# Five operations of a decoder layer kernel moved to other places in their engines' queues

## The chip, the cores and the metric

The kernel runs on one core of a Trainium2 chip. The metric is the device time of one execution in microseconds (us). The kernel before took 818.10 us (median of three runs, 817.72 to 818.36).

A core has five engines, each with its own queue of instructions that is worked off in order: TensorE (PE, matrix products; its loading of weights is shown apart as PEld), VectorE (DVE), ScalarE (ACT), GpSimd (POOL) and SyncE (SP, which here only starts DMA transfers). An engine waits for another by a semaphore. A wait holds back everything behind it in that engine's queue.

## The reference

One layer of a decoder, for 512 tokens of width 1024, in float32:

```python
proj = x @ w_in                                  # q | k | v (3 groups x 8 heads x 64) | ssm input (512) | gates
for g, (window, dilation) in enumerate(DILATION_GROUPS):       # (128,1), (512,4), (2048,16)
    o_g, lse_g = dilated_group_attention(rope(q)[g], rope(k)[g], v[g], window, dilation)
attn = sum(softmax(lses) * outs);  y_attn = attn @ w_attn_br
y_s = s5_ssm(u, ...)                             # complex diagonal state space, scan over the tokens
y_s = glu(gelu(y_s) @ w_glu);      y_ssm = y_s @ w_ssm_br
mixed = sigmoid(gates[0]) * y_attn + sigmoid(gates[1]) * y_ssm
h = layer_norm(ALPHA * x + mixed @ w_out)
ff = (silu(h @ w_ff_gate) * (h @ w_ff_up)) @ w_ff_down
out = layer_norm(ALPHA * h + ff)
```

## The kernel before

Every matrix product of float32 data is made of three products of reduced numbers. A number is split into a high part (a cast to a shorter format, on ACT: names ending in `h`, `_hi` or `whi`) and a low part (the number less its high part, a subtraction on DVE: `l`, `_lo`, `wlo`), and PE adds high x high, high x low and low x high into one PSUM bank. A weight therefore goes through a DMA into a raw buffer, a cast on ACT and a subtraction on DVE before PE can use it. A class `Weights` does this in the order of use, one 128x1024 half at a time; a finished product releases its slot, and the release queues the next half's cast and subtraction. `w.flush()` emits a subtraction that has been put off.

The order of the work is written out by hand. Python code emits instructions product by product, and a table of steps (`at_step`) says at which product other pieces (the state space, scores, norms) are put in between. Each engine's queue holds its instructions in the order of emission. There is no scheduler.

The places that the change touches, in order of time:

**The first product** (`u_tiles`, line L613). Input and weights arrive in eight k-slices of 512 columns. A loop splits each slice: ACT casts the input (`x_hi`) and then the weight (`wuh`), DVE subtracts (`x_lo`, `wul`). Between slices DVE takes a few of the state space's small operations (`late.take`; their tiles are `t16s`, their line is L79). Slice 0 was split in halves ahead of the loop.

**The state space's output** (`ssm_out`, `ssm_gelu`). It is made in two rounds. `ssm_out(rnd)` is a short burst of products in the middle of a projection's product: `yt` (banks 3, 4; L724) and `yc` (banks 5, 6; L732). `ssm_gelu(rnd)` is emitted half a step later, behind that projection's own evictions: ACT copies `yt` into `ysb`, DVE adds `yc` to it, and the GELU follows on ACT and DVE. Both rounds use the same four banks. Between them on DVE stand the rotary products of one eviction (`kq`, `zk`) and a weight's subtraction (`wlo`).

**The values of the far groups** (`v_product(n, u)`, L1213). These are seven products of a Strassen scheme, in the order n = 1, 5, 2, 6, 3, 7, 4, each in two halves u. A half is 12 matmuls of 128x512 into two banks (e = 0, 1), with two k-slices and three terms. The input's forms are made on the way: form 5 is an `x_hi`, `x_lo` pair that is cast on ACT and subtracted on DVE; forms 6 and 7 (`x23h`, `x23l`) need a DMA that adds into `xf`. After the second half `v_evict(n)` copies or adds the banks out.

**The last of the quads** (`quad_product(j, n)`, L1257; j = 0 to 4, n in the order 1, 5, 6, 2, 7, 3, 4). Products 1, 6, 7 and 4 add up in one bank. After each, `quad_evict` reads what the bank holds. In the last quad the reading of product 7 is an addition to `qssw` on DVE (L348) and two tanh activations on ACT (L1268). In the loop the slot's release stands ahead of this reading, so the next weight's cast and subtraction are queued first.

**The last norm.** The 512 tokens are four tiles of 128. A tile's norm takes its two halves of 512 columns, with two operations on each: `norm_first` is (z - mean) * gain, `norm_second` is z * rstd + bias, both on DVE (L345). For tiles 0 and 1 the second half is shared out (`normalize_shared`): ACT computes z * rstd + nm, where `nm` = -mean * rstd, and POOL multiplies by the gain (L1457) and adds the bias (L1458). `rstd` is computed on POOL (L1431). For tile 2 all four operations are DVE's; in front of them in time is tile 3's first quarter, behind them the rest of tile 3 (`dnv`, the last product's bank), its norm and the last stores.

Of the kernel before, what the change touches and what calls it, by code (L numbers as in the profile page):

```python
# [10 lines left out]
F32 = mybir.dt.float32  # L11
F32R = mybir.dt.float32r
I32 = mybir.dt.int32
AF = mybir.ActivationFunctionType
ALU = mybir.AluOpType

P = 128
# [19 lines left out]
QUADS = [(1, 0), (1, 1), (2, 0), (2, 1), (None, 3)]  # L37
# [136 lines left out]
def emit(ctx, tc, i, out):  # L174
    nc = tc.nc
    pe, dve, act, pool, sp = nc.tensor, nc.vector, nc.scalar, nc.gpsimd, nc.sync
# [22 lines left out]
    def split(hi, lo, src, scale=None):  # L199
        if scale is None:  # L200
            act.copy(hi, src)  # L201
            dve.tensor_tensor(lo, src, hi.bitcast(F32), op=ALU.subtract)  # L202
        else:
            act.mul(hi, src, scale)
            dve.scalar_tensor_tensor(lo, src, scale, hi.bitcast(F32), op0=ALU.mult, op1=ALU.subtract)
# [18 lines left out]
    at = pa_ctx.enter_context(tc.tile_pool(name="at", bufs=2))  # L224
# [12 lines left out]
    def gat(n, name, dt=F32):  # L237
        return pa.tile([P, 2048], dt, tag=f"gat{n}", name=name)
# [13 lines left out]
    for n in range(2, N_GLU, 2):  # L252
        kind, g, un, _ = STEPS[n]
# [43 lines left out]
    for n, c in enumerate(cols256):  # L297

        xs, us = (raws[0][:, 0, 2 * n + e] for e in range(2))
# [29 lines left out]
    late = Later(dve)  # L329
# [8 lines left out]
    def ts(o, a, s1, op0, s2=None, op1=None, eng=dve):  # L338
        if s2 is None:
            eng.tensor_scalar(o, a, s1, None, op0=op0)  # L340
        else:
            eng.tensor_scalar(o, a, s1, s2, op0=op0, op1=op1)

    def stt(o, a, s1, b, op0, op1, eng=dve):
        eng.scalar_tensor_tensor(o, a, s1, b, op0=op0, op1=op1)  # L345

    def tt(o, a, b, op, eng=dve):
        eng.tensor_tensor(o, a, b, op=op)  # L348
# [148 lines left out]
    for k in range(KT):  # L497
        (xh, uh), (xl, ul) = ((z[k // 4][:, k % 4, :] for z in (xp[n], wup[n])) for n in range(2))
        raw = raws[k // 2][:, k % 2]
        if k == 0:  # L500
            late.take(4)
            continue
        for n, (hi, lo) in enumerate(((xh, xl), (uh, ul))):
            split(hi, lo, raw[:, 2 * n : 2 * n + 2].rearrange("p e c -> p (e c)"))
        late.take(4 if k < 2 else 10)


    xt = []
# [36 lines left out]
    ssm = {}  # L545
# [165 lines left out]
    def ssm_out(rnd):  # L711

        if rnd == 0:
            late.take(1000)
            ssm["ysb"] = gat(0, "ysb").rearrange("p (a i b c) -> p a i b c", a=2, i=4, b=2)
        ut, h, y = ssm["ut"], ssm["h"], ssm["ysb"]
        tb, cb = ([ring_(f"y{n}{rnd}{e}").rearrange("p (o i c) -> p o i c", o=2, i=2) for e in range(2)]
                  for ring_, n in ((scores, "t"), (turned, "c")))
        for e in range(2):
            for par in range(2):  # L720
                for half, rows in halves64:
                    for x, cols in halves64:
                        i_ = 4 * rnd + 2 * e + x
                        pe.matmul(tb[half][cols, par, e], ssm["tm"][rows, 2 * i_ + par, :], ut[rows, 2 * i_ + par, :],  # L724
                                  start=True, stop=True)
        for e in range(2):
            for half in range(2):
                for r in range(2):
                    for par, rows in halves64:
                        for x, cols in halves64:  # L730
                            i_ = 4 * rnd + 2 * e + x
                            pe.matmul(cb[par][cols, half, e], caf[rows, i_, r, half, :], h[r][rows, 2 * i_ + half, :],  # L732
                                      start=(r == 0), stop=(r == 1))
        ssm["yb"] = tb, cb

    def ssm_gelu(rnd):
        y, (tb, cb) = ssm["ysb"], ssm["yb"]
        is_ = slice(2 * rnd, 2 * rnd + 2)
        yf = [y[:, half, is_].rearrange("p i b c -> p (i b c)") for half in range(2)]
        y2 = [at.tile([P, 512], F32, tag="un", name=f"y2_{rnd}{half}", bufs=4) for half in range(2)]  # L740
        for half in range(2):
            for par in range(2):
                act.copy(y[:, half, is_, par], tb[half][:, par])
                tt(y[:, half, is_, par], y[:, half, is_, par], cb[par][:, half], ALU.add)
        for a, b in zip(y2, yf):
            act.square(a, b)
            ts(a, a, 0.044715, ALU.mult, 1.0, ALU.add)
            tt(a, a, b, ALU.mult)
        for a, b in zip(y2, yf):
            act.activation(a, a, AF.Tanh, scale=math.sqrt(2.0 / math.pi))  # L750
            stt(b, a, 1.0, b, ALU.add, ALU.mult)
# [452 lines left out]
    def v_product(n, u):  # L1204
        key = {1: "x", 6: "x", 7: "x", 4: "x", 2: "y", 5: "z", 3: "z"}[n]
        first = n in (1, 2, 5) and u == 0
        if first:
            vbank[key] = [bank(b, f"v{key}{b}") for b in {"x": (0, 7), "y": (1, 2), "z": (5, 6)}[key]]
        ws, xs = vops.pop((n, u)), forms_x["f"][n]
        for e in range(2):  # L1210
            for kk in range(2):
                for m, (p_, q_) in enumerate(((0, 0), (0, 1), (1, 0))):
                    pe.matmul(vbank[key][e], xs[p_][:, 2 * u + kk, 128 * e : 128 * e + 128], ws[q_][:, kk, :],  # L1213
                              start=(first and kk == m == 0), stop=(kk == 1 and m == 2), skip_group_check=True)

# [64 lines left out]
    def quad_evict(j, n):  # L1280
        if n == 1 and j == 0:
            z = home("g2", "qsnap")
            qsnap.update({m: z[:, 512 * e : 512 * e + 512] for e, m in enumerate((1, 5, 6))})
        elif n == 1 and QUADS[j][0] is None:
            a, b = (at.tile([P, 2, 512], F32, tag=t, name=f"qs{t}", bufs=1) for t in ("sw", "cq"))
            qsnap.update({1: a[:, 0], 5: a[:, 1], 6: b[:, 0]})
        x, y, z = (qbank.get(k) for k in "xyz")
        s = qsnap
        if n in (1, 5, 6):
            act.copy(s[n], z if n == 5 else x)  # L1290
        elif n == 2:
            tt(s[1], s[1], y, ALU.add)
            quad_out(j, 0, 0, s[1])
        elif n == 7:
            tt(s[5], s[5], x, ALU.add)
            quad_out(j, 1, 1, s[5])
        elif n == 3:
            tt(s[6], s[6], z, ALU.add)
            quad_out(j, 0, 1, s[6])
        else:  # L1300
            quad_out(j, 1, 0, x)
# [12 lines left out]
    for n in range(4, N_GLU):  # L1314
        kind, g, un, c = STEPS[n]
# [33 lines left out]
    for j in range(len(QUADS)):  # L1349
        for m, n in enumerate(QORDER):  # L1350
            now = QUAD_AT + 4 * j + 4 * m / 7
            if any(k <= now for k in fill):
                w.flush()
            run_fill(now)
            if (j, m) == (0, 0):
                w.extra, w.extra_ok = extra, lambda _: len(qnext) > 3
                assert all(p is not None for p, _ in w.free)
                w.free.append((None, 0))
                w.split()
            quad_product(j, n)  # L1360
            w.held.appendleft(qslot.pop((j, n)))
            w.release()
            quad_evict(j, n)

    gh_, gl_ = (home(j, f"g{n}", F32R).rearrange("p (q t) -> p q t", q=4) for j, n in (("g0", "h"), (2, "l")))
    glu, brs = ring(0, 1, 2), ring(2, 3, 0, 1)
    for n in range(4):
        ws = w.views[N_GLU + n]
        bs = []
        for e in range(2):  # L1370
            b = glu(f"gl{n}{e}")
# [14 lines left out]
    for n in range(8):  # L1386
# [23 lines left out]
        if n >= 4:  # L1410
            for ch, t0, _ in ts_:
                hi, lo = kslice(mx, ch)
# [7 lines left out]
    bt = ctx.enter_context(tc.tile_pool(name="bt", bufs=2))  # L1420
# [4 lines left out]
    hn = [hns[t // 2][:, t % 2, :] for t in range(NTT)]  # L1425
# [7 lines left out]
    def norm_first(z, mv, ln, cs):  # L1433
        stt(z[:, cs], z[:, cs], mv[:, 0:1], ln[:, 0, cs], ALU.subtract, ALU.mult)

    def norm_second(z, mv, ln, cs):
        stt(z[:, cs], z[:, cs], mv[:, 3:4], ln[:, 1, cs], ALU.mult, ALU.add)

    halves = [slice(512 * e, 512 * e + 512) for e in range(2)]
# [92 lines left out]
    mvs = [bt.tile([P, 4], F32, name=f"mva{t}", bufs=1) for t in range(NTT)]  # L1532
# [166 lines left out]
    half = [slice(1024 * e, 1024 * e + 1024) for e in range(2)]  # L1699
# [124 lines left out]
    hn = [hns[t // 2][:, t % 2, :] for t in range(NTT)]  # L1824
# [15 lines left out]
    mvs = [bt.tile([P, 4], F32, name=f"mvb{t}", bufs=1) for t in range(NTT)]  # L1840
# [53 lines left out]
    lnb2 = late_["lnb2"]  # L1894
# [11 lines left out]
    z = hn[2][:, halves[0]]  # L1906
# [5 lines left out]
    z = hn[3][:, 0:256]  # L1912
    stt(z, z, ALPHA, acc["x"][1][:, 0:256], ALU.mult, ALU.add)
    dve.bn_stats(bsts[3][:, 0, :], z)
    norm_second(hn[2], mvs[2], lnb2, halves[0])
    norm_first(hn[2], mvs[2], lnb2, halves[1])
    norm_second(hn[2], mvs[2], lnb2, halves[1])
    for e in halves:
        store((sp, sp), 2, hn[2], e)
    keys[4] = "v"  # L1920
# [2 lines left out]
    z = hn[3][:, cs]  # L1923
# [116 lines left out]
```

## Time and profile before

The profiled execution took 818.33 us, 0.23 us above the median of the runs. Its span, from the first to the last instruction, is 816.5 us.

| engine | busy, us | share of the span | instructions |
|---|---|---|---|
| PE | 803.8 | 98% | 5584 |
| PEld | 721.8 | 88% | 5584 |
| DVE | 667.2 | 82% | 1059 |
| ACT | 411.9 | 50% | 607 |
| POOL | 80.3 | 10% | 98 |

The mean granted TensorE clock is 0.996 of full speed. In rows of the timeline a line starts with the start time and the busy time in us, then engine, line, operation, written tile <- read tiles, shape and count; a row with xN is N instructions run together, its busy time that of the whole. In square brackets stands how long the engine was idle before, and what ended that. Successive matmuls overlap in these rows, so PE's pace is read from one start to the next.

### The profile page before, as it was taken

Reading aid. Unit: us, or ns where it says so; the run is one execution under the profiler, and the core shown is the slowest. Engines: PE = TensorE matmul, PEld = TensorE weight load, DVE = VectorE, ACT = ScalarE, POOL = GpSimd, SP = SyncE. Lnnn points to the kernel's source line nnn. Section 1 sums busy time; section 2 is a strip of 40 time slices with the busy share of each in tenths; the row PEclk is TensorE's granted clock in tenths of the full one; section 3 lists DMA queues with packets and bytes.
Section 4 is the critical chain, followed back from the end, with each engine's and each line's share of the span. In section 5 each row is a group of like instructions: output and inputs, shape, how many; then the busy total and the mean of one; then the engine's idle time right before and its main releaser. Section 6 shows DMA issues by size and latency. Waiting matters only on the chain.

```text
span 816.5 us, 13783 instructions
## 1 busy us (share of the span) xinstructions
PE 803.8 (98%) x5584; PEld 721.8 (88%) x5584; DVE 667.2 (82%) x1059; ACT 411.9 (50%) x607; POOL 80.3 (10%) x98
## 2 busy tenths in 40 slices
PE   9999999999999999999999999999999999999995
PEld 7888888878899999988888899999999999888884
DVE  7977997989787799556896698877777789789986
ACT  6973222637576645874233355455555556555520
POOL 0000002230011333000000420000000000010104
PEclk9999999999999999999999999999999999999998
DMA  8733447695035654651624143332222323765454
GB/s 339 195 112 102 144 148 231 187 203 152 28 110 124 134 106 112 229 199 52 258 89 170 51 163 148 116 137 107 107 104 104 105 104 133 274 142 168 136 127 104
DMA packets 32048, 117.49 MB, mean 144 GB/s; under 512 B 7664, under 2 KB 12528, under 8 KB 22512
## 3 DMA queue, kind: packets, MB, share of 16 engines
q1 hardware_dynamic: 23808, 91.83, 32.4%
q0 software_dynamic: 6544, 23.07, 13.6%
q10 hardware_dynamic: 1632, 1.70, 0.6%
q8 instruction: 44, 0.72, 0.4%
q14 instruction: 20, 0.16, 0.1%
HBM read 100.60 MB, written 9.70 MB: 135 GB/s over the span
## 4 chain that ended last, share of the span: by engine, by line
PE 89%; DVE 5%; ACT 2%; issue 1%; POOL 1%; DMA 1%; DVEq 0%; SPq 0%; ACTq 0%
PE qx L1257 7%; PE dnx L1797 5%; PE dnz L1797 4%; PE qz L1257 3%; PE pg L208 3%; PE pg L209 3%; PE pg L210 3%; PE pu L613 2%; PE dny L1797 2%; PE wo L210 2%; PE wo L209 2%; PE b L210 2%; PE b L209 2%; PE wo L208 2%; PE b L208 2%; PE s L836 2%
## 5 line engine op out<-in xcount | busy, mean ns | idle before, releaser
L1597 ACT CAST whi<-sums 128x1024 fp32r<-128x1024 f32 x40 | 41.9, 1048 | 66.2 <-DVE sums L348 66.2
L202 DVE TENSOR_TENSOR wlo<-raw,whi 128x1024 fp32r<-128x1024 f32 x44 | 54.1, 1233 | 18.0 <-ACT whi L201 18.0
L201 ACT CAST whi<-raw 128x1024 fp32r<-128x1024 f32 x44 | 45.8, 1046 | 23.5 <-PE pk L209 17.4
L348 DVE TENSOR_TENSOR wlo<-sums,whi 128x1024 fp32r<-128x1024 f32 x40 | 48.8, 1220 | 0.0
L1152 ACT CAST whi_q<-rq 128x1024 fp32r<-128x1024 f32 x28 | 29.3, 1051 | 35.8 <-DVE rq L348 25.0
L348 DVE TENSOR_TENSOR wlo_q<-rq,whi_q 128x1024 fp32r<-128x1024 f32 x28 | 34.2, 1221 | 15.5 <-ACT whi_q L1152 15.4
L1797 PE MATMUL dnx<-whi_d,pc 128*128 128x512 f32 (+1 forms) x128 | 38.2, 376 | 0.0
L849 ACT ACTIVATE un<-un,st 128x256 f32<-128x256 f32 (+1 forms) x64 | 30.8, 484 | 13.6 <-DVE st L847 13.6
L208 PE MATMUL pg<-x_hi,whi 128*128 128x512 f32 x96 | 37.6, 392 | 0.0
L209 PE MATMUL pg<-x_lo,whi 128*128 128x512 f32 x96 | 37.4, 390 | 0.0
L210 PE MATMUL pg<-x_hi,wlo 128*128 128x512 f32 x96 | 37.4, 389 | 0.0
L774 POOL DMA_DIRECT2D kq<-qz x32 | 25.3, 1748 | 111.6 <-ACT un L861 70.6
L964 ACT ACTIVATE gt<-pg,bgate 128x512 f32<-128x512 f32 x12 | 8.3, 690 | 41.8 <-PE pg L210 41.8
L1709 ACT CAST whi_d<-dn 128x1024 fp32r<-128x1024 f32 x16 | 16.9, 1053 | 22.8 <-DVE dn L348 10.9
L1797 PEld LDWEIGHTS dnx<-whi_d,pc 128*128 128x128 f32 x128 | 23.6, 188 | 4.4
L1719 POOL DMA_DIRECT2D whi_db<-in_w_dp x3 | 1.7, 577 | 246.1 <-PE dny L1797 242.4
L348 DVE TENSOR_TENSOR wlo<-ra,whi 128x1024 fp32r<-128x1024 f32 x20 | 24.4, 1220 | 0.4 <-ACT whi L1597 0.4
L1797 PE MATMUL dnx<-wlo_d,pc 128*128 128x512 f32 (+1 forms) x64 | 24.1, 376 | 0.0
L1257 PE MATMUL qx<-x23h,whi_q 128*128 128x256 f32 x80 | 23.1, 289 | 0.0
L1257 PE MATMUL qz<-x_hi,whi_q 128*128 128x256 f32 x80 | 22.9, 287 | 0.0
L1257 PE MATMUL qz<-x_hi,wlo_q 128*128 128x256 f32 x80 | 22.6, 283 | 0.0
L1257 PE MATMUL qx<-x23h,wlo_q 128*128 128x256 f32 x80 | 22.6, 283 | 0.0
(842 smaller groups left out, 2978.0 us busy)
## 6 DMA issues: line engine op xcount, KB each, us to landing
raw<-in_w_in SPq DMA_DIRECT2D x12, 1024.0 KB, 5.4
ra<-in_w_gu SPq DMA_DIRECT2D x10, 1024.0 KB, 4.8
rb<-in_w_gu SPq DMA_DIRECT2D x10, 1024.0 KB, 4.9
rq<-in_w_quad SPq DMA_DIRECT2D x16, 512.0 KB, 4.3
dn<-in_w_dq SPq DMA_DIRECT2D x8, 1024.0 KB, 4.9
rv<-in_w_in SPq DMA_DIRECT2D x4, 1024.0 KB, 9.2
kq<-qz POOLq DMA_DIRECT2D x32, 128.0 KB, 5.7
raw<-in_w_br SPq DMA_DIRECT2D x4, 1024.0 KB, 4.8
```

The lines of the kernel that those rows point to most:

```text
L201: act.copy(hi, src)
L202: dve.tensor_tensor(lo, src, hi.bitcast(F32), op=ALU.subtract)
L208: pe.matmul(dst, a[0], b[0], start=first, stop=False)
L209: pe.matmul(dst, a[0], b[1], start=False, stop=False)
L210: pe.matmul(dst, a[1], b[0], start=False, stop=last)
L348: eng.tensor_tensor(o, a, b, op=op)
L774: pool.dma_start(dst[32 * q : 32 * q + 32], z[32 * (q ^ 1) : 32 * (q ^ 1) + 32], accum_op=ALU.add)
L849: act.activation(pt, pt, AF.Exp, bias=mneg, scale=-1.0, accum_out=zsum)
L1152: act.copy(hi, src)
L1257: pe.matmul(d[:, 256 * e : 256 * e + 256], p_[:, e, k, :], q_[:, k, :], start=(first and e == k == m == 0), stop=(k == 3 and m == 2), skip ...
L1597: act.copy(hi, src)
L1797: pe.matmul(acc[key][0 if key == "v" else e][:, cs], p_, q_[:, cs], start=(key, e) not in begun, stop=(m == 2), skip_group_check=True)
```

## The change

Five edits, each at one of the places above.

1. In the split of slice 1 the weight's cast `wuh` goes from ACT to DVE, and the eight small operations of slices 0 and 1 are all taken behind the slice's split (they were taken four and four, ahead of it and behind it).
2. The four copies and four additions of the state space's output move from `ssm_gelu` to the end of `ssm_out`, directly behind the products they read.
3. `v_product` runs over the three terms in its outer loop: four matmuls of high x high, then four with the weight's low part, then four with the input's low part. Before, each group of three matmuls had all three.
4. For product 7 of the last quad, the reading of the bank is emitted ahead of the slot's release instead of behind it.
5. Of tile 2's norm, the last 256 columns go the way of tiles 0 and 1: `nm` on DVE, one activation on ACT, a multiplication and an addition on POOL. DVE does the columns 512 to 768 as before, in two operations of 256 columns.

```diff
         if k == 0:
-            late.take(4)
             continue
-        for n, (hi, lo) in enumerate(((xh, xl), (uh, ul))):
-            split(hi, lo, raw[:, 2 * n : 2 * n + 2].rearrange("p e c -> p (e c)"))
-        late.take(4 if k < 2 else 10)
+        xs, us = (raw[:, 2 * n : 2 * n + 2].rearrange("p e c -> p (e c)") for n in range(2))
+        if k == 1:
+            act.copy(xh, xs)
+            dve.tensor_copy(uh, us)
+            tt(xl, xs, xh.bitcast(F32), ALU.subtract)
+            tt(ul, us, uh.bitcast(F32), ALU.subtract)
+            late.take(8)
+            continue
+        split(xh, xl, xs)
+        split(uh, ul, us)
+        late.take(10)
...
-        ssm["yb"] = tb, cb
-
-    def ssm_gelu(rnd):
-        y, (tb, cb) = ssm["ysb"], ssm["yb"]
+
         is_ = slice(2 * rnd, 2 * rnd + 2)
-        yf = [...]
-        y2 = [...]
         for half in range(2):
             for par in range(2):
                 act.copy(y[:, half, is_, par], tb[half][:, par])
                 tt(y[:, half, is_, par], y[:, half, is_, par], cb[par][:, half], ALU.add)
+
+    def ssm_gelu(rnd):
+        y = ssm["ysb"]
...
-        for e in range(2):
-            for kk in range(2):
-                for m, (p_, q_) in enumerate(((0, 0), (0, 1), (1, 0))):
+        for m, (p_, q_) in enumerate(((0, 0), (0, 1), (1, 0))):
+            for e in range(2):
+                for kk in range(2):
                     pe.matmul(vbank[key][e], xs[p_][:, 2 * u + kk, 128 * e : 128 * e + 128], ws[q_][:, kk, :],
...
             w.held.appendleft(qslot.pop((j, n)))
+            last = (j, n) == (len(QUADS) - 1, 7)
+            if last:
+                quad_evict(j, n)
             w.release()
-            quad_evict(j, n)
+            if not last:
+                quad_evict(j, n)
...
+    ends = [slice(512, 768), slice(768, 1024)]
+    nm = bt.tile([P, 1], F32, tag="nm", name="nm")
+    stt(nm, mvs[2][:, 0:1], -1.0, mvs[2][:, 3:4], ALU.mult, ALU.mult)
     norm_second(hn[2], mvs[2], lnb2, halves[0])
-    norm_first(hn[2], mvs[2], lnb2, halves[1])
-    norm_second(hn[2], mvs[2], lnb2, halves[1])
+    norm_first(hn[2], mvs[2], lnb2, ends[0])
+    norm_second(hn[2], mvs[2], lnb2, ends[0])
+    z = hn[2][:, ends[1]]
+    act.activation(z, z, AF.Identity, bias=nm, scale=mvs[2][:, 3:4])
+    pool.tensor_tensor(z, z, lnb2[:, 0, ends[1]], op=ALU.mult)
+    pool.tensor_tensor(z, z, lnb2[:, 1, ends[1]], op=ALU.add)
     for e in halves:
         store((sp, sp), 2, hn[2], e)
```

How the queues stand at three of these places follows; a row gives the line, the operation, written tile <- read tiles, and the shape, and numbers behind a name tell buffers apart. First DVE's queue between the two rounds of the state space's output before the change (`yc_1421`, `yc_1422` are the first round's banks, `pk_1405` is a projection's, `y_00` the first round's GELU):

```order
L202 TENSOR_TENSOR wlo_24_1402<-raw_1295,whi_24_1401 128x1024
L348 TENSOR_TENSOR kq_1484<-pk_1405,rope 128x4x128
L348 TENSOR_TENSOR zk_1483<-pk_1405,rope 128x4x128
L202 TENSOR_TENSOR wlo_25_1488<-raw_1295,whi_25_1487 128x1024
L348 TENSOR_TENSOR ysb<-ysb,yc_1421 128x2x128
L348 TENSOR_TENSOR ysb<-ysb,yc_1422 128x2x128
...
L342 TENSOR_SCALAR y_00_1493<-y_00_1493 128x512
```

and the same piece after it:

```order
L202 TENSOR_TENSOR wlo_24_1402<-raw_1295,whi_24_1401 128x1024
L348 TENSOR_TENSOR ysb<-ysb,yc_1421 128x2x128
L348 TENSOR_TENSOR ysb<-ysb,yc_1422 128x2x128
...
L348 TENSOR_TENSOR kq_1492<-pk_1405,rope 128x4x128
L348 TENSOR_TENSOR zk_1491<-pk_1405,rope 128x4x128
L202 TENSOR_TENSOR wlo_25_1496<-raw_1295,whi_25_1495 128x1024
L342 TENSOR_SCALAR y_00_1501<-y_00_1501 128x512
```

The additions (four; two are left out) moved ahead of two rotary products and a subtraction; on ACT the four copies moved ahead of the cast of `whi_25` in the same way, and the second round's copies and additions moved likewise.

Second, PE's queue at the first half of product 5 of the far values (`vz_1836` and `vz_1837` are its two banks), before:

```order
L1213 MATMUL vz_1836<-whi_v_1717,x_hi_93 128x512
L1213 MATMUL vz_1836<-wlo_v_1718,x_hi_93 128x512
L1213 MATMUL vz_1836<-whi_v_1717,x_lo_95 128x512
...
L1213 MATMUL vz_1837<-whi_v_1717,x_hi_93 128x512
L1213 MATMUL vz_1837<-wlo_v_1718,x_hi_93 128x512
L1213 MATMUL vz_1837<-whi_v_1717,x_lo_95 128x512
```

and after:

```order
L1221 MATMUL vz_1836<-whi_v_1717,x_hi_93 128x512 x2
L1221 MATMUL vz_1837<-whi_v_1717,x_hi_93 128x512 x2
L1221 MATMUL vz_1836<-wlo_v_1718,x_hi_93 128x512 x2
L1221 MATMUL vz_1837<-wlo_v_1718,x_hi_93 128x512 x2
L1221 MATMUL vz_1836<-whi_v_1717,x_lo_95 128x512 x2
L1221 MATMUL vz_1837<-whi_v_1717,x_lo_95 128x512 x2
```

The low part of the weight (`wlo_v`) is first read by the fifth matmul instead of the second, the low part of the input (`x_lo`) by the ninth instead of the third.

Third, DVE's queue in the last norm (`mvb_7168` and `hr_7069` are tile 2's statistics and its buffer, `dnv` is the last product's bank), before:

```order
L1914 BN_STATS bstb_7165<-hr_7069 128x6
L345 SCALAR_TENSOR_TENSOR hr_7069<-hr_7069,mvb_7168,lnb_7647 128x512 x3
L348 TENSOR_TENSOR hr_7069<-hr_7069,dnv_7900 128x256
L1925 BN_STATS bstb_7165<-hr_7069 128x6
L1853 BN_AGGR mvb_7169<-bstb_7165 128x2
```

and after:

```order
L1926 BN_STATS bstb_7165<-hr_7069 128x6
L345 SCALAR_TENSOR_TENSOR nm<-mvb_7168 128x1
L345 SCALAR_TENSOR_TENSOR hr_7069<-hr_7069,mvb_7168,lnb_7647 128x512
L345 SCALAR_TENSOR_TENSOR hr_7069<-hr_7069,mvb_7168,lnb_7647 128x256 x2
L348 TENSOR_TENSOR hr_7069<-hr_7069,dnv_7905 128x256
L1944 BN_STATS bstb_7165<-hr_7069 128x6
```

Three operations of 512 columns became one of one column, one of 512 and two of 256; on POOL two operations of 128x256 were added between tile 2's `rstd` and tile 3's.

More of the change, by code (lines that the diff above doesn't have):

```diff
@@ L733, in ssm_out @@
                                       start=(r == 0), stop=(r == 1))
-        ssm["yb"] = tb, cb
-    def ssm_gelu(rnd):
-        y, (tb, cb) = ssm["ysb"], ssm["yb"]
         is_ = slice(2 * rnd, 2 * rnd + 2)
-        yf = [y[:, half, is_].rearrange("p i b c -> p (i b c)") for half in range(2)]
-        y2 = [at.tile([P, 512], F32, tag="un", name=f"y2_{rnd}{half}", bufs=4) for half in range(2)]
         for half in range(2):
@@ L744, in ssm_gelu @@
                 tt(y[:, half, is_, par], y[:, half, is_, par], cb[par][:, half], ALU.add)
+    def ssm_gelu(rnd):
+        y = ssm["ysb"]
+        is_ = slice(2 * rnd, 2 * rnd + 2)
+        yf = [y[:, half, is_].rearrange("p i b c -> p (i b c)") for half in range(2)]
+        y2 = [at.tile([P, 512], F32, tag="un", name=f"y2_{rnd}{half}", bufs=4) for half in range(2)]
         for a, b in zip(y2, yf):
```

## The prediction

> **What bounds the kernel now.** I read the page first, then the list of PE's waits, then PE's timeline around each wait, and last the timelines of the engines that ended them.
>
> ```profile
> PE 803.8 (98%) x5584; PEld 721.8 (88%) x5584; DVE 667.2 (82%) x1059; ACT 411.9 (50%) x607; POOL 80.3 (10%) x98
> PE vz L1213 <- DVE x_lo L348: 0.5, 1, 0.5
> PE yc L732 <- DVE ysb L348: 0.5, 1, 0.5
> PE qx L1257 <- DVE qssw L348: 0.4, 1, 0.4
> PE pu L613 <- ACT wuh L201: 0.4, 1, 0.4
> ```
>
> PE sets the end: it is busy 98% of the span, and of its idle time the waits above are nearly all that lies inside the run. They are four, and four of the five edits stand at these four places. The list understates them, because a matmul's recorded end lies behind the start of the next one. So I take each loss from start to start, against an undisturbed stretch of the same instructions. The fifth edit stands behind PE's last matmul, where DVE sets the end.
>
> **Edit 1, the first weights' cast.** ACT casts the input, then the weight, and PE needs both:
>
> ```profile
> 6.80 0.62 ACT L201 CAST x_hi<-raw_x 128x512 fp32r<-128x512 f32 x1 [2.09 <-DMA raw_x<-in_xw]
> 7.32 0.61 ACT L201 CAST wuh<-raw_x 128x512 fp32r<-128x512 f32 x1
> 7.01 0.62 PE L613 MATMUL pu<-x_hi,wul 128*128 128x512 f32 x2
> 7.99 1.20 PE L613 MATMUL pu<-x_hi,wuh 128*128 128x512 f32 x4 [0.36 <-ACT wuh L201]
> 3.52 0.29 DVE L302 CAST wuh<-raw_x 128x256 fp32r<-128x256 f32 x1 [2.52 <-DMA raw_x<-in_xw]
> ```
>
> The weight's cast ends at 7.93 and PE starts at 7.99. On DVE the cast starts with the data at 6.80. The same cast at half the width took 0.29 there, so at 512 columns it takes between 0.29 and 0.58 and ends by 7.38 at the latest. The input's cast ends at 7.42 either way, so it comes last, and PE starts at about 7.48. That is also when the two matmuls from 7.01 have gone in (7.01 + 2 x 0.23). The gain is 7.99 - 7.48 = 0.51. DVE was idle at 6.80 but for the small operations, which go behind the split; they feed nothing that PE reads in this product.
>
> **Edit 2, the state output's additions.** The second round's `yc` needs its banks back, and these are read late:
>
> ```profile
> 136.18 1.10 PE L724 MATMUL yt<-ut,tm 64*64 64x128 f32 x32
> 138.96 0.50 PE L208 MATMUL pk<-x_hi,whi 128*128 128x512 f32 x1
> 144.66 1.10 PE L724 MATMUL yt<-ut,tm 64*64 64x128 f32 x32
> 148.48 0.50 PE L208 MATMUL pk<-x_hi,whi 128*128 128x512 f32 x1
> 142.05 1.09 DVE L348 TENSOR_TENSOR kq<-pk,rope 128x512 f32<-128x512 f32 x1 [4.41 <-PE pk L210]
> 145.04 1.40 DVE L348 TENSOR_TENSOR ysb<-ysb,yc 128x256 f32<-128x256 f32 x4
> 142.79 1.17 ACT L743 COPY ysb<-yt 128x256 f32<-128x256 f32 x4
> ```
>
> The first round's burst takes 138.96 - 136.18 = 2.78 from its start to the next projection matmul, the second 148.48 - 144.66 = 3.82. The wait costs 1.04. The first round's `yc` is done at about 139.0, and DVE is idle then (4.41 until 142.05). There the additions take 1.40 and end near 140.5, 5 us before the second `yc`. The copies on ACT (1.17) go ahead of a cast that itself waits for PE until about 141.8, so they delay nothing. What is queued behind the moved additions on DVE, `kq`, waits for PE until 142.05 anyway. In the second round the additions stand between the first GELU's last step and the next `kq`, in an idle stretch of DVE as well, so DVE's later chain also comes forward, by up to 1.04 + 1.40. I take 1.04. If DVE's cover were gone, 1.40 would come back.
>
> **Edit 3, the far values' term order.**
>
> ```profile
> 178.53 0.39 PE L1213 MATMUL vz<-whi_v,x_hi 128*128 128x512 f32 x1
> 179.67 0.50 PE L1213 MATMUL vz<-whi_v,x_lo 128*128 128x512 f32 x1 [0.52 <-DVE x_lo L348]
> 184.79 0.39 PE L1213 MATMUL vy<-whi_v,x_hi 128*128 128x512 f32 x1
> 195.67 0.39 PE L1213 MATMUL vz<-whi_v,x_hi 128*128 128x512 f32 x1
> 201.49 0.39 PE L1213 MATMUL vx<-whi_v,x23h 128*128 128x512 f32 x1
> 194.87 1.22 DVE L348 TENSOR_TENSOR wlo_v<-rv,whi_v 128x1024 fp32r<-128x1024 f32 x1
> 184.05 1.05 ACT L1099 CAST x23h<-xf 128x1024 fp32r<-128x1024 f32 x1 [6.92 <-DMA xf<-in_xk]
> ```
>
> Products 2 and 6 run undisturbed from 184.79 to 195.67, 5.44 each, or 0.227 a matmul. Product 5 takes 184.79 - 178.53 = 6.26, 0.82 too long, and waits for `x_lo`. Product 3 takes 201.49 - 195.67 = 5.82, 0.38 too long: its `wlo_v` is ready at 196.09 and is wanted by the second matmul. In the new order `x_lo` is wanted by the ninth matmul instead of the third, 6 x 0.227 = 1.36 later, and `wlo_v` by the fifth instead of the second, 0.68 later. Both grants exceed the lateness, so both losses go: 1.20. The number of matmuls and weight loads is the same. The bank e = 0 is finished 4 matmuls (0.9) later than before at each end. What waits for it are evictions, and the only tight one, product 7's before product 4, has a block of scores of 1.7 us in between. PE comes to this stage 1.55 earlier by edits 1 and 2, which shrinks the margins; DVE comes earlier by about as much or more, so I leave the 1.20 whole.
>
> **Edit 4, the last quad's read.**
>
> ```profile
> 330.29 1.91 PE L859 MATMUL t<-ident,un 128*128 128x128 f32 x16
> 331.96 0.36 PE L1257 MATMUL qy<-x_hi,wx_q 128*128 128x256 f32 x1
> 344.73 1.91 PE L859 MATMUL t<-ident,un 128*128 128x128 f32 x16
> 347.03 0.51 PE L1257 MATMUL qx<-x,whi_q 128*128 128x256 f32 x2 [0.39 <-DVE qssw L348]
> 345.15 1.23 DVE L202 TENSOR_TENSOR wlo<-raw,whi 128x1024 fp32r<-128x1024 f32 x1 [0.24 <-ACT whi L201]
> 346.30 0.68 DVE L348 TENSOR_TENSOR qssw<-qssw,qx 128x512 f32<-128x512 f32 x1
> 347.01 0.91 ACT L1268 ACTIVATE gt<-qssw,bgate 128x256 f32<-128x256 f32 x2 [1.89 <-DVE qssw L348]
> 350.01 0.40 PE L208 MATMUL gl<-yh,whi 128*128 128x512 f32 x1
> ```
>
> The block `t` takes 331.96 - 330.29 = 1.67 undisturbed and 347.03 - 344.73 = 2.30 here: 0.63 lost. The reading of product 7 stands behind the subtraction that ends at 346.38. DVE is free for it from 344.91 (0.24 idle before 345.15), so ahead of the subtraction it ends at 345.6, while `t` still runs until 346.4. What is late next is that weight. Its cast on ACT now stands behind the two tanh steps (0.91, so until 346.5) and takes 1.05, as the cast of the same size at 184.05 above; the subtraction follows until about 348.8. PE wants this low part at the third matmul of `gl`, at 350.01 + 2 x 0.23 - 0.63 = 349.84. So 1.0 of cover is left, and the gain is 0.63.
>
> **Edit 5, the third tile's norm.** DVE's arithmetic alone says a gain: three operations in 2.12 (805.17 to 807.29) become 0.71 + 0.36 + 0.36 and 0.12 for `nm`, 1.55, so that `dnv` is added at 806.73, just as PE is done (806.40 + 0.28), 0.55 sooner.
>
> ```profile
> 805.17 2.20 DVE L345 SCALAR_TENSOR_TENSOR hr<-hr,mvb,lnb 128x512 f32<-128x512 f32 x3 [0.44 <-POOL mvb L1431]
> 807.29 0.41 DVE L348 TENSOR_TENSOR hr<-hr,dnv 128x256 f32<-128x256 f32 x1
> 806.40 0.28 PE L1797 MATMUL dnv<-whi_d,pc 128*128 128x256 f32 x1
> 797.33 0.82 ACT L1456 ACTIVATE hr<-hr,nm,mvb 128x512 f32<-128x512 f32 x1 [6.30 <-DVE nm L345]
> 797.26 1.42 DVE L345 SCALAR_TENSOR_TENSOR hr<-hr,mvb,lnb 128x512 f32<-128x512 f32 x2
> 798.22 1.60 POOL L1457 TENSOR_TENSOR hr<-hr,lnb 128x512 f32<-128x512 f32 x1 [0.59 <-ACT hr L1456]
> 798.59 1.25 DVE L345 SCALAR_TENSOR_TENSOR nm<-mvb 128x1 f32<-128x1 f32 x1
> 801.62 1.28 POOL L1457 TENSOR_TENSOR hr<-hr,lnb 128x512 f32<-128x512 f32 x1
> ```
>
> But the rows of tiles 0 and 1 show POOL and DVE shutting each other out. POOL's multiplication takes 1.28 alone and 1.60 when DVE's norm runs at its start. DVE's `nm`, one column, takes 1.25 and ends (799.84) when POOL does (799.82). POOL, which had waited since 798.22, went ahead of the `nm` that was next in DVE's queue. The Trainium skill says why: GPSIMD Engine Reference, section Specifications, has GpSimd share its SBUF interfaces with VectorE and contend with VectorE instructions that have two SBUF inputs. By this rule the edit gains nothing or loses, by plain addition of durations it gains 0.55; the rows agree with the rule.
>
> In the new tail `nm` ends at 805.29. ACT's 256 columns take between 0.41 and 0.82 (half of the 512 row, and all of it), I take 0.6, and POOL asks near 806.0, just as DVE has begun the first short operation. POOL goes next at about 806.3, for between 0.64 (half of 1.28) and 1.28; I take 0.7. DVE's second short operation waits till 807.0 and ends near 807.3. So `dnv` is added at 807.3 as before: 0.0. If ACT is quick, POOL gets in twice and it costs 0.6; if POOL comes after both, it gains 0.55. Both ends go into the range.
>
> **Sum.** 0.51 + 1.04 + 1.20 + 0.63 + 0.0 = 3.38. From the profiled 818.33 that is 814.95; the median of the runs lies 0.23 lower, so 814.7.
>
> **Rivals.** *The chain behind a DMA pins the far values.* The last row of edit 3's fence is the cast of `x23h`, which a DMA into `xf` holds up until 184.05. From there DVE works almost without a break to the `wlo_v` of 194.87. If the transfer lands no earlier though everything before it does, that `wlo_v` still ends at 196.09 and product 3 can start no earlier than 196.09 - 4 x 0.227 = 195.18. Then edits 1 to 3 together bring 195.67 + 0.38 - 195.18 = 0.87, and with edit 4's 0.63 the time is 816.6. Against it: the transfer is issued behind DVE's chain, which edit 2 brings forward. *Slower than before:* the same place, with the transfer landing later than now because it meets the state output's stores at another moment. Each us past 184.05 costs one; from 185.55 the 1.50 is used up, and at 186.5 the time is 819.0. Nothing in the rows makes it later by that much. *Partial:* an early gain is lost between 10 and 140 us, where DVE is nearly full, or edit 4's cast becomes late; one of the terms of 0.5 to 1.0 is missing, 815.6. *The edit to the tail does something after all:* 814.1 or 815.3.
>
> **How the numbers follow.** Forecast with the tail unchanged 0.56, tail otherwise 0.16, partial 0.15, pinned 0.10, slower 0.03. No change means within 0.2%, 1.6 us, about what a measurement of this kernel can tell; 816.5 is the border. Faster: the first three cases, 0.87. Same: the pinned one, 0.10. Slower 0.03. The range reaches from below the better tail, 814.0, to 816.3, short of the pinned case. The forecast's own is 814.1 to 815.3.
>
> **What would show it.** In the new profile, PE's list of waits has none of the four rows, or much smaller ones; the second burst of `yt` and `yc` takes 2.8; products 5 and 3 take 5.44; the block before the last `qx` 1.7; product `qx` there starts 3.4 earlier (343.6). From the last PE row to the end nothing changes by over 0.1, and DVE's second short operation is recorded at 0.9 to 1.0 beside POOL. A wait for `wlo` at `gl`, or for `x23h` or `wlo_v` at products 6, 3 or 7, would make it wrong.

## The result and the profile after

The changed kernel took 815.03 us (median of six runs, 814.72 to 815.46) beside 817.93 us for the kernel before (six runs, 817.72 to 818.65). The ratio is 0.9963 with a 95% interval of 0.9951 to 0.9976. The forecast was 814.7 with a range of 814.0 to 816.3: a gain of 3.4, of which 2.9 came. The profiled executions have spans of 813.6 and 816.5.

The page and the list of PE's waits of the changed kernel, which answer to the first fence of the prediction:

```profile
PE 802.8 (99%) x5584; PEld 722.4 (89%) x5584; DVE 667.4 (82%) x1061; ACT 411.8 (51%) x607; POOL 82.1 (10%) x100
PE warm_b L292 <- DVE warm L288: 1.1, 1, 1.1
```

All four waits are gone; what is left is the wait for the cleared operand ahead of the first warm-up matmul. PE's timeline of the changed kernel shows the five places from start to start:

```profile
8.13 1.08 PE L620 MATMUL pu<-x_hi,wuh 128*128 128x512 f32 x4
136.21 1.10 PE L731 MATMUL yt<-ut,tm 64*64 64x128 f32 x32
144.70 1.10 PE L731 MATMUL yt<-ut,tm 64*64 64x128 f32 x32
147.48 0.50 PE L208 MATMUL pk<-x_hi,whi 128*128 128x512 f32 x1
177.57 1.07 PE L1221 MATMUL vz<-whi_v,x_hi 128*128 128x512 f32 x4
183.01 1.07 PE L1221 MATMUL vy<-whi_v,x_hi 128*128 128x512 f32 x4
193.90 1.07 PE L1221 MATMUL vz<-whi_v,x_hi 128*128 128x512 f32 x4
199.34 0.84 PE L1221 MATMUL vx<-whi_v,x23h 128*128 128x512 f32 x3
342.57 1.91 PE L867 MATMUL t<-ident,un 128*128 128x128 f32 x16
344.23 0.48 PE L1265 MATMUL qx<-x,whi_q 128*128 128x256 f32 x2
803.56 0.28 PE L1809 MATMUL dnv<-whi_d,pc 128*128 128x256 f32 x1
```

Each row against its counterpart before gives how far PE is ahead, and the steps between give the gain of each place:

| place | before, us | after, us | ahead, us | gained here, us | forecast, us |
|---|---|---|---|---|---|
| k = 1 group starts | 7.99 | 8.13 | -0.14 | | |
| first `yt` | 136.18 | 136.21 | -0.03 | -0.03 (edit 1) | 0.51 |
| `pk` behind the second burst | 148.48 | 147.48 | 1.00 | 1.03 (edit 2's place) | 1.04 |
| product 2, behind product 5 | 184.79 | 183.01 | 1.78 | 0.82 (edit 3's place) | 0.82 |
| product 7, behind product 3 | 201.49 | 199.34 | 2.15 | 0.38 (edit 3's place) | 0.38 |
| `qx` of the last quad | 347.03 | 344.23 | 2.80 | 0.65 (edit 4's place) | 0.63 |
| last matmul | 806.40 | 803.56 | 2.84 | | |
| `dnv` added | 807.29 | 804.34 | 2.95 | 0.11 (edit 5's place) | 0.0 |

The k = 1 group is the four matmuls at 8.13, the first that need the weights of slice 1. Ahead is the difference of the two starts; a gain is what it grows by across that place (product 5 itself starts 0.96 ahead, product 3 1.77). Four of the five places did what was forecast to about 0.1. The first did nothing, though the wait that it was to remove is gone. And a gain at a place is not yet a gain by the edit that stands there; that needs the experiments.

### The profile page after: what moved, and what is told of

It reads as the page before. It is cut to its first block, busy times and chain, and to the rows that moved or that the text cites. A ratio compares the mean times of both kernels' runs of the same rounds, so it can differ in the third digit from the quotient of the medians.

```text
span 813.6 us, 13794 instructions
## 1 busy us (share of the span) xinstructions
PE 802.8 (99%) x5584; PEld 722.4 (89%) x5584; DVE 667.4 (82%) x1061; ACT 411.8 (51%) x607; POOL 82.1 (10%) x100
## 4 chain that ended last, share of the span: by engine, by line
PE 97%; POOL 1%; DVE 1%; issue 0%; ACT 0%; DVEq 0%; POOLq 0%
PE qx L1265 7%; PE dnx L1809 5%; PE dnz L1809 4%; PE qz L1265 4%; PE pu L620 3%; PE pg L208 3%; PE vx L1221 3%; PE pg L209 3%; PE pg L210 3%; PE dny L1809 2%; PE s L844 2%; PE wo L208 2%; PE wo L209 2%; PE b L209 2%; PE b L208 2%; PE wo L210 2%
## 5 line engine op out<-in xcount | busy, mean ns | idle before, releaser
L201 ACT CAST whi<-raw 128x1024 fp32r<-128x1024 f32 x44 | 45.8, 1046 | 18.7 <-PE pk L209 11.3
```

## The experiments

Medians of neighbouring kernels overlap here (the intervals are about 1 us wide on either side), so single terms are read from start to start in the profiles, and times with intervals are given where a kernel ran several times.

### Which edit frees the far values

One run takes edit 3 out of the change, one makes edit 2 alone, one edit 3 alone, and one takes edit 2 out. The edit of the first, in `v_product` (the second and third are hunks 2 and 3 of the diff above alone):

```diff
-        for m, (p_, q_) in enumerate(((0, 0), (0, 1), (1, 0))):
-            for e in range(2):
-                for kk in range(2):
+        for e in range(2):
+            for kk in range(2):
+                for m, (p_, q_) in enumerate(((0, 0), (0, 1), (1, 0))):
```

> The changed kernel with the far values' products in the old term order; the other four edits stay. Theory of the prediction (edit 3 is what frees product 5 and product 3): both waits come back, product 5 takes 6.26 from its start to the next product's start and product 3 takes 5.82, and the span is 813.6 + 1.2 = 814.8. Rival (edit 2, by bringing VectorE's chain forward, had already freed both: in the changed kernel x_lo is done at 177.7 and the old order wants it at 177.57 + 0.46 = 178.03; wlo_v is done at 192.2 and is wanted at 194.13): both products take 5.44 and the span stays at 813.6 within 0.2.

> The kernel before with edit 2 alone (the state output's additions behind each round). Theory of the prediction (the terms add up, edit 2 is worth 1.04): the second burst takes 2.8, products 5 and 3 still take about 6.26 and 5.82, and the span is 816.5 - 1.04 = 815.5. Rival (edit 2 moves VectorE's chain by up to 2.4 and so frees products 5 and 3 as well): these two take 5.44 and the span is 816.5 - 1.04 - 1.20 = 814.3.

> The kernel before with edit 3 alone (the far values' term order). Theory of the prediction: products 5 and 3 take 5.44 each, span 816.5 - 1.20 = 815.3. Rival (without edit 2 the transfer into xf lands at about 184 as before, and the chain of casts and subtractions from there holds product 3's wlo_v until 196.09): product 5 takes 5.44, product 3 starts at 194.85 and waits about 0.3 at its fifth matmul, span 816.5 - 0.87 = 815.6.

> The changed kernel with the state output's additions back behind the second burst; edits 1, 3, 4 and 5 stay. Theory of the prediction (terms add up): only edit 2's term comes back, the second burst takes 3.8, products 5 and 3 take 5.44, span 813.6 + 1.04 = 814.6. Theory after the last runs (edit 2's earlier VectorE chain is what freed products 5 and 3; edit 3's order cannot, because x23h is cast only when the transfer into xf has landed near 184.3): product 5 takes 5.44, product 3 about 6.5, span 813.6 + 1.04 + 1.1 = 815.7.

PE's timeline of the change without edit 3, where products 5, 2, 3 and 7 begin (6 is left out):

```profile
176.85 0.39 PE L1221 MATMUL vz<-whi_v,x_hi 128*128 128x512 f32 x1
182.29 0.39 PE L1221 MATMUL vy<-whi_v,x_hi 128*128 128x512 f32 x1
...
193.18 0.39 PE L1221 MATMUL vz<-whi_v,x_hi 128*128 128x512 f32 x1
198.62 0.39 PE L1221 MATMUL vx<-whi_v,x23h 128*128 128x512 f32 x1
```

In the old term order products 5 and 3 take 5.44 each, and 2 and 6 together 10.89. The span is 812.9 and the ratio to before 0.9958 (0.9941 to 0.9975): nothing is lost without edit 3. Edit 2 alone has the same; its product 5 and the start of product 2 read:

```profile
177.72 0.39 PE L1214 MATMUL vz<-whi_v,x_hi 128*128 128x512 f32 x1
183.16 0.39 PE L1214 MATMUL vy<-whi_v,x_hi 128*128 128x512 f32 x1
```

Products 5 and 3 take 5.44 (177.72 to 183.16) and 5.45 (194.04 to 199.49), the span is 814.5, the ratio 0.9971 (0.9960 to 0.9982). In both comparisons the rival's times came true and the prediction's did not.

Edit 3 alone, PE's timeline and ACT's:

```profile
178.39 1.07 PE L1213 MATMUL vz<-whi_v,x_hi 128*128 128x512 f32 x4
183.83 1.07 PE L1213 MATMUL vy<-whi_v,x_hi 128*128 128x512 f32 x4
194.71 1.07 PE L1213 MATMUL vz<-whi_v,x_hi 128*128 128x512 f32 x4
196.58 1.19 PE L1213 MATMUL vz<-wlo_v,x_hi 128*128 128x512 f32 x4 [0.81 <-DVE wlo_v L348]
201.25 1.07 PE L1213 MATMUL vx<-whi_v,x23h 128*128 128x512 f32 x4
184.48 1.05 ACT L1099 CAST x23h<-xf 128x1024 fp32r<-128x1024 f32 x1 [7.50 <-DMA xf<-in_xk]
```

Product 5 takes 5.44, so the new order does cover `x_lo`. But product 3 takes 201.25 - 194.71 = 6.54, and from product 5's start to product 7's it is 22.86 against 22.96 before: 0.10 gained in place of 1.20. The span is 816.4, the ratio 0.9990 (0.9981 to 0.9999). The change without edit 2 shows the same place with the transfer a little sooner:

```profile
183.88 1.05 ACT L1106 CAST x23h<-xf 128x1024 fp32r<-128x1024 f32 x1 [6.88 <-DMA xf<-in_xk]
194.73 1.07 PE L1220 MATMUL vz<-whi_v,x_hi 128*128 128x512 f32 x4
195.98 1.19 PE L1220 MATMUL vz<-wlo_v,x_hi 128*128 128x512 f32 x4 [0.18 <-DVE wlo_v L348]
```

From the cast of `x23h` to the matmul that wants product 3's `wlo_v` it is 12.10 in both (196.58 - 184.48, 195.98 - 183.88), and before the `wlo_v` ended at 196.09, 12.04 behind the cast at 184.05. So the chain from the landing has a fixed length, and without edit 2 it alone says when product 3 goes on. That is the pinned rival of the prediction. The span without edit 2 is 814.9 and the median ratio 0.9967 (0.9954 to 0.9980), between the two expectations of 814.6 and 815.7.

Why edit 2 unpins it stands in POOL's issue of the transfer that this cast waits for. Before (the cast at 184.05 stands in the prediction), and then in the change with its cast:

```profile
172.68 0.93 POOL L1085 DMA_DIRECT2D xf<-in_xk  x1 [1.98 <-ACT xf L1084]
```

```profile
170.38 0.92 POOL L1093 DMA_DIRECT2D xf<-in_xk  x1 [1.99 <-ACT xf L1092]
180.16 1.05 ACT L1107 CAST x23h<-xf 128x1024 fp32r<-128x1024 f32 x1 [4.00 <-DMA xf<-in_xk]
```

The issue comes 2.30 sooner, about the 1.04 + 1.40 by which the prediction let VectorE's chain come forward. In all profiles the issue stands between 169.6 and 171.6 with edit 2 and between 172.5 and 172.7 without. For product 5 no transfer is needed: DVE starts its `x_lo` at 176.47 in place of 178.41, 1.94 sooner, while PE comes 0.96 sooner. The way from issue to cast is 11.4 and 9.8 here; over the runs it lies between 9.1 and 12.1 with edit 2 and between 11.3 and 12.8 without, and why it varies is not settled. With edit 2 the cast starts between 179.2 and 182.7 in all profiles, without it between 183.9 and 185.4. At 180.2 the `wlo_v` is there by 192.3, and even the old order wants it only at 193.90 + 0.23.

### The last quad's read

> The changed kernel with the last quad's read behind the release again. Theory of the prediction: product 7's read goes behind the subtraction of the next weight, the block t takes 2.3 instead of 1.67, PE waits for qssw, and the span is 813.6 + 0.6 = 814.2. Rival (VectorE's earlier chain of edits 2 and 3 had freed this place too): the block takes 1.7 and the span stays at 813.6 within 0.2.

```diff
-            last = (j, n) == (len(QUADS) - 1, 7)
-            if last:
-                quad_evict(j, n)
             w.release()
-            if not last:
-                quad_evict(j, n)
+            quad_evict(j, n)
```

PE's and DVE's timelines of the change without edit 4:

```profile
342.82 1.91 PE L867 MATMUL t<-ident,un 128*128 128x128 f32 x16
345.11 0.51 PE L1265 MATMUL qx<-x,whi_q 128*128 128x256 f32 x2 [0.39 <-DVE qssw L348]
343.24 1.22 DVE L202 TENSOR_TENSOR wlo<-raw,whi 128x1024 fp32r<-128x1024 f32 x1 [0.25 <-ACT whi L201]
344.38 0.68 DVE L348 TENSOR_TENSOR qssw<-qssw,qx 128x512 f32<-128x512 f32 x1
```

The block takes 2.29 again, 0.63 more than the 1.66 of the change. This place is not freed by what comes before it: the subtraction and the read are tied to the last product of the quad and come forward with PE. The prediction's term stands. The span is 814.5, of which 0.28 is a later k = 1 group (8.41 against 8.13).

### When the first weights' cast is worth something

The rows of `pu` at the start explain the missing 0.51. PE's timeline of the change, then of the change without edit 3, which is the same kernel up to here:

```profile
5.49 0.63 PE L620 MATMUL pu<-x_hi,wuh 128*128 128x256 f32 x2
5.91 0.63 PE L620 MATMUL pu<-x_lo,wuh 128*128 128x256 f32 x2
...
6.74 0.63 PE L620 MATMUL pu<-x_hi,wuh 128*128 128x512 f32 x2
```

```profile
5.12 0.40 PE L620 MATMUL pu<-x_hi,wuh 128*128 128x256 f32 x2
5.36 0.40 PE L620 MATMUL pu<-x_lo,wuh 128*128 128x256 f32 x2
...
7.30 1.20 PE L620 MATMUL pu<-x_hi,wuh 128*128 128x512 f32 x4
```

The same pairs start 0.42 apart in one execution and 0.24 in the other. PE begins at about half pace, and the trace says when it changes over: in its list of granted clock the first entry, full clock, starts at 6.70 in the first and at 4.08 in the second; in the kernel before it was 5.19. (In the second, the pairs up to 5.12 are still 0.32 to 0.34 apart: PE has caught up with DVE there, whose subtractions end at 4.38 and 4.73, just ahead of the pairs that read them at 4.45 and 4.78.) The late change costs 0.66 against the kernel before by the start of the 512 columns (6.74 against 6.08), more than the 0.51 that edit 1 was to gain. The table by windows does not show it; a microsecond of it reads, in the change and before:

```profile
5.00:6.00 1.00, 1.00 (x7) 1.00 (x6) 0.41 (x2) 0.00 (x0) 0.00 (x0) 1.00 1.00 325
```

```profile
5.00:6.00 1.00, 1.00 (x10) 1.00 (x9) 0.42 (x2) 0.00 (x0) 0.00 (x0) 1.00 0.91 299
```

PE is busy throughout and the clock (third number from the end) stands at 1.00 in both, but 7 matmuls are recorded in one and 10 in the other. The 1.00 is no measurement here: the table counts time ahead of the first entry as full clock.

Edit 1 alone was run, and two kernels that are meant to bring a late change of pace by cutting the warm-up, with and without edit 1 (one execution of each):

```diff
-    for n in (3, 3, 1):
+    for n in (1,):
```

> The kernel before with edit 1 alone (the first weights' cast on VectorE). Theory (the gain depends on when PE's matmuls begin to go at full pace): where the pairs of 128x256 matmuls go 0.24 us apart from about 5.3 on, the k = 1 group starts near 7.3 to 7.5, against 7.83 and 7.99 without the edit; where they go 0.43 apart until about 6.7, it starts at 8.1 to 8.4, as without the edit (8.29). Rival (the edit is worth 0.51 whatever the pace): 7.5 or, at the slow pace, 7.8.

> The changed kernel with its three idle warm-up matmuls ahead of the first product cut to one of 128 columns (their result is never read). Theory (PE's first matmuls go at half pace until it has been busy for some us, and then edit 1 finds nothing to gain): the 12 matmuls of 256 columns take 0.21 each and at least some of the 6 of 512 columns 0.43, so PE comes to the k = 1 group at 8.0 to 9.2, behind the cast in either version, and that group starts without a wait. Rival (the pace does not depend on PE's earlier work): the pace changes between 4.8 and 7 as in the other runs.

> The same without edit 1 (ScalarE casts the k = 1 weights behind the input, done near 7.9). Theory: the k = 1 group starts at 8.0 to 9.2 as in the kernel with edit 1, without a wait for the cast; the edit is worth nothing here. Rival (the edit is worth about 0.5 at any pace): 0.5 later than with it.

PE's timelines with the warm-up cut, first with edit 1, then without it:

```profile
8.51 1.04 PE L620 MATMUL pu<-x_hi,wul 128*128 128x512 f32 x2
9.36 1.11 PE L620 MATMUL pu<-x_hi,wuh 128*128 128x512 f32 x4
```

```profile
7.93 0.62 PE L613 MATMUL pu<-x_hi,wul 128*128 128x512 f32 x2
8.39 1.07 PE L613 MATMUL pu<-x_hi,wuh 128*128 128x512 f32 x4
```

Neither waits for the cast: the k = 1 group follows the pair before it at PE's own distance. The one with edit 1 starts even later, at 9.36, because full clock came only there, at 9.41 against 7.21. The spans follow, 814.8 and 813.8: the start pace alone was worth 1 us of the span here.

All profiled executions fit one reading. With full clock from 4.0 to 5.5 on, the k = 1 group starts at 7.83 and 7.99 without edit 1 (two executions), and at 7.30 to 7.60 with it (five). With full clock from 6.4 or later it starts at 8.0 or later, with the edit (8.02, 8.13, 8.41, and 9.36 above) as without (8.29, and 8.39 above). One lies between (full clock at 6.1, with the edit, 7.97). So edit 1 is worth about 0.5 in one kind of execution and nothing in the other.

Edit 1 alone showed where the stall goes next. Its k = 1 group started at 7.46, but the first `yt` at 136.09, only 0.09 ahead of before: the data of k = 2 landed late, ACT's cast of them started at 9.42 (2.01 us waiting for the DMA), and the k = 2 group waited for it until 10.61. Its span of 817.9 is longer than before because `x23h` was cast at 185.38 in this execution, which holds product 6 by 0.33 and product 3 by 1.03 longer than before. A single execution with a late landing does not show that the edit alone makes the kernel slower.

### What the tail's 0.1 is made of

> The changed kernel without GpSimd's two operations on the third tile (its last 256 columns are left without the scale and the offset). Theory (GpSimd's multiplication goes between VectorE's two short operations and makes the second wait): the three merged operations of VectorE take about 1.4 instead of 2.01, and dnv is added 0.28 to 0.35 after the start of PE's last matmul instead of 0.78, as soon as PE is done. Rival (VectorE's operations take this long by themselves): 2.01 and 0.78 as now.

```diff
-    pool.tensor_tensor(z, z, lnb2[:, 0, ends[1]], op=ALU.mult)
-    pool.tensor_tensor(z, z, lnb2[:, 1, ends[1]], op=ALU.add)
```

The tail of the change, on DVE, ACT, and POOL:

```profile
802.33 0.16 DVE L345 SCALAR_TENSOR_TENSOR nm<-mvb 128x1 f32<-128x1 f32 x1 [0.44 <-POOL mvb L1443]
802.40 2.01 DVE L345 SCALAR_TENSOR_TENSOR hr<-hr,mvb,lnb 128x512 f32<-128x512 f32 x3
804.34 0.41 DVE L348 TENSOR_TENSOR hr<-hr,dnv 128x256 f32<-128x256 f32 x1
802.52 0.60 ACT L1934 ACTIVATE hr<-hr,nm,mvb 128x256 f32<-128x256 f32 x1 [4.68 <-DVE nm L345]
803.20 0.93 POOL L1935 TENSOR_TENSOR hr<-hr,lnb 128x256 f32<-128x256 f32 x1 [0.91 <-ACT hr L1934]
```

The same without POOL's two operations:

```profile
801.73 1.66 DVE L345 SCALAR_TENSOR_TENSOR hr<-hr,mvb,lnb 128x512 f32<-128x512 f32 x3
803.31 0.41 DVE L348 TENSOR_TENSOR hr<-hr,dnv 128x256 f32<-128x256 f32 x1
802.88 0.28 PE L1809 MATMUL dnv<-whi_d,pc 128*128 128x256 f32 x1
```

DVE's three operations take 1.66 in place of 2.01, and `dnv` is added 0.43 behind the start of PE's last matmul in place of 0.78 (804.34 - 803.56). So 0.35 is the price of POOL's two operations next to them, and it lies where the theory has it: DVE's second short operation is recorded at 0.83 with them and at 0.48 without. And 1.66 rather than 1.4 is DVE's own time: an operation of 256 columns takes more than half of 512 columns (0.47 in the row below).

From this follows a version that keeps POOL out of the way. The first short operation needs only the mean, so it goes into the 0.44 in which DVE waits for POOL's `rstd`; and the second one goes ahead of the 512 columns, so that POOL asks when DVE's last operation on this tile already runs:

```diff
+    norm_first(hn[2], mvs[2], lnb2, ends[0])
     nm = bt.tile([P, 1], F32, tag="nm", name="nm")
     stt(nm, mvs[2][:, 0:1], -1.0, mvs[2][:, 3:4], ALU.mult, ALU.mult)
-    norm_second(hn[2], mvs[2], lnb2, halves[0])
-    norm_first(hn[2], mvs[2], lnb2, ends[0])
     norm_second(hn[2], mvs[2], lnb2, ends[0])
+    norm_second(hn[2], mvs[2], lnb2, halves[0])
```

> The changed kernel with the third tile's first short operation ahead of nm, in the 0.44 us in which VectorE waits for GpSimd's power, and the second short operation ahead of the 512 columns: GpSimd then asks while the last of VectorE's operations on this tile runs. Theory (the lock of the two engines costs only what stands between them): VectorE is done about 1.2 after nm starts, dnv is added 0.3 to 0.4 after the start of PE's last matmul instead of 0.78, and the end comes 0.4 sooner than in the changed kernel, span 813.2 for the same start. Rival (GpSimd gets in between once more, or the additional operation delays nm): 0.78 or more, span 813.6 or above.

> The changed kernel once more, beside the next run on the same chip. Theory: from the start of PE's last matmul to the addition of dnv 0.78; the k = 1 group starts near 7.4 if PE's pace changes before 5.5 and near 8.2 if it changes after 6.5, and the span is 812.9 in the first case, 813.6 in the second.

> The kernel with the third tile's short operations put around the wait, once more beside the change. Theory: 0.32 from the start of PE's last matmul to the addition of dnv, 0.46 less than in the change; span 812.4 or 813.1 by the pace of the start, and the median 0.4 to 0.5 below that of the change, which the runs can just about tell. Rival (the end is set by something else): the same time as the change.

Its tail, DVE, then POOL and PE:

```profile
801.07 0.47 DVE L345 SCALAR_TENSOR_TENSOR hr<-hr,mvb,lnb 128x256 f32<-128x256 f32 x1
801.68 1.14 DVE L345 SCALAR_TENSOR_TENSOR hr<-hr,mvb,lnb 128x256 f32<-128x256 f32 x2
803.15 0.42 DVE L348 TENSOR_TENSOR hr<-hr,dnv 128x256 f32<-128x256 f32 x1 [0.33 <-PE dnv L1809]
802.48 0.93 POOL L1935 TENSOR_TENSOR hr<-hr,lnb 128x256 f32<-128x256 f32 x1 [0.91 <-ACT hr L1934]
802.83 0.28 PE L1809 MATMUL dnv<-whi_d,pc 128*128 128x256 f32 x1
```

DVE now waits 0.33 for PE, and `dnv` is added 0.32 behind PE's last start: 0.46 won, in both executions. The medians are 814.42 (ratio 0.9947, interval 0.9935 to 0.9960) and 814.57 (0.9951, 0.9938 to 0.9965), beside 815.28 for the change on the same chip as the second (0.9958, 0.9946 to 0.9971). This is the fastest version; the intervals overlap, so that it beats the change rests on the two tails. Of the 0.9 between the spans of that pair (812.6 and 813.5), 0.46 is the tail and 0.42 the pace at the start (the k = 1 group at 7.60 and 8.02).

## Why the prediction was nearly right, and for partly other reasons

**Edit 1 is the term that was mis-sized**: 0.51 forecast, -0.03 in this pair. The step that failed is "That is also when the two matmuls from 7.01 have gone in (7.01 + 2 x 0.23)". It took PE's arrival at 7.48 as given, and PE's arrival depends on when full clock begins, at 5.19 in the profile before and at 6.70 in the one after. There PE came at 8.13, behind both casts. Where full clock begins early, the gain is there: the first `yt` starts at 135.47 to 135.66 with the edit (edit 1 alone aside) and at 136.02 and 136.18 without; one such execution, the change without edit 3 at 812.9, stands 3.6 ahead of the profiled one before.

**Edit 2's own term was right, and its reach too small**: 1.04 forecast, 1.03 measured. The sentence "so DVE's later chain also comes forward, by up to 1.04 + 1.40" was right as well (2.30 at the issue of `xf`), but nothing was made of it in the sum. Edit 2 alone is worth its burst and 1.20 at products 5 and 3.

**Edit 3's term has the right size at the wrong edit.** The step that failed is "Both grants exceed the lateness, so both losses go: 1.20". The grants do exceed the lateness of before, but with edit 2 there is none left: taking edit 3 out costs nothing, and alone it brings 0.10. The total was not touched, since the sum counted the two stalls once; that it came out is luck as far as edit 3 goes. What edit 3 still buys is cover for a late transfer: in the run without POOL's two operations `x23h` was cast at 181.79, so `wlo_v` would be ready at about 193.9, and the old order would want it at 193.21 + 0.23. This 0.4 is worked out, not run.

**The pinned rival is how the kernel works without edit 2.** Its argument "the transfer is issued behind DVE's chain, which edit 2 brings forward" is what kept it from happening. Its price was put at 0.87 for edits 1 to 3 together; with edit 3 alone the far values gained 0.10, with 1, 3, 4 and 5 they gained 0.72 (22.24 from product 5 to product 7), by where the landing fell. The rival of a slower kernel was set aside because "Nothing in the rows makes it later by that much"; with edit 1 alone the cast came at 185.38, 1.33 later than before and 0.17 short of the 185.55 of that rival.

**Edit 4** held: 0.65 measured, 0.63 forecast. The weight that is late next ended at 346.73 and was wanted at 347.65, a cover of 0.9 where 1.0 was forecast.

**Edit 5** held to 0.11. ACT took the assumed 0.60, POOL went between DVE's two short operations, and the second waited (it is recorded at 0.83, where 0.9 to 1.0 was forecast). The lock was priced too high and the short operations too low, and by luck the two nearly cancelled: 0.35 and 1.66 were measured for the waiting and for DVE's own three operations, against 0.7 and 1.43. The Trainium skill's sentence on the shared interfaces (GPSIMD Engine Reference, section Specifications) agrees: 0.35 went when POOL's operations did.

## What to carry to other kernels

When two edits stand on one chain of work, ask of the later one whether its stall is still there once the earlier is made; the sum of the stalls is the same, but only taking each edit out says which to keep. A stall in the first microseconds has to be priced at more than one start pace of PE, which is read from the distance between matmuls. Two engines that lock each other out are best given their work so that the one asks while the last operation of the other already runs.

## What the runs showed of the hardware that was not expected

PE's first matmuls go at half pace (0.43 us between pairs of 256 columns, then 0.24). This is the granted clock. The trace's list of it has no entry for the start and one of full clock behind it, and in the profiled executions PE's distances change within one or two matmuls of where that entry starts, save in two where it starts ahead of the first pair. For the same warm-up from 1.06 us on it starts at 4.00 to 7.27, 2.9 to 6.2 us later. With the warm-up cut and PE steadily busy only from 4.11 it starts at 7.21 and 9.41, 3.1 and 5.3 us later. The clock in the views is 1.00 over this time, and the mean of 0.996 of the kernel before leaves the slow start out: it comes from an entry of half clock from 810.74 us on, behind PE's last matmul. The entry of full clock lasts 798.72, 802.13 or 805.55 us, so from run to run its length moves in steps of 3.41 us.

The Trainium skill (TensorE: Matmul & The Clock Gate, section Part 1: The HAM clock gate) describes a clock that starts at half rate and is released after a busy window of about 3.4 us, which runs freely and so catches each run at another phase. The steps of 3.41 us agree with such a window, and so does a spread of 3.3 us (4.00 to 7.27). The section's own spread of half a microsecond to either side does not agree, and the measurement decides.
